# Long feed-forward blocks with their output pieces two and two instead of three and one, and three of the four prepared by adding transfers

## The chip, the cores and the metric

The kernel runs on one core of a Trainium2 chip. The metric is the device time of one execution in microseconds (us); lower is better. Before the change the median of three runs is 2339.63 us (2338.91 to 2342.2).

The core has engines that run side by side, each with its own queue of instructions: TensorE (PE, with its weight loads shown apart as PEld), VectorE (DVE), ScalarE (ACT), GpSimd (POOL) and SyncE (SP). Here SP and POOL mostly issue DMA transfers, which 16 DMA engines carry out.

## The reference

One decoder layer on 256 tokens of width 2048, all in float32. Two SwiGLU feed-forward networks (FFN) stand around a token mixer:

```python
def swiglu(h, w_in, w_out):
    a, b = jnp.split(h @ w_in, 2, axis=-1)
    return (jax.nn.silu(a) * b) @ w_out

h = layer_norm(DN_ALPHA * h + 0.5 * swiglu(h, ffn1_w_in, ffn1_w_out), ln1_g, ln1_b)
...
h = layer_norm(DN_ALPHA * h + merged @ w_out, ln2_g, ln2_b)
h = layer_norm(DN_ALPHA * h + 0.5 * swiglu(h, ffn2_w_in, ffn2_w_out), ln3_g, ln3_b)
```

`w_in` of an FFN is 2048 x 11264, `w_out` is 5632 x 2048. Between the two FFNs stand sparse attention, a gated linear recurrence and their merge; the change does not touch the text of that part. (The mixer's pieces go through the same class of weights.)

## The kernel before

**Three products for one.** TensorE multiplies a rounded float32 format. To keep float32 accuracy every operand is split into a high part (the value rounded) and a low part (what the rounding left out), and a product takes three matmuls: high by high, high by low, low by high (`three`, lines 742 to 745). Activations are split once and kept. Weights stream from memory and are split as they come, in pieces of 128 x 1024 (512 KB).

**How a piece is split.** `Weights` holds the list of all pieces in the order in which TensorE uses them. There are three ways:

- A plain piece: SP loads it into a `raw` tile (four buffers), ACT copies it into the high half of an `hl` tile (five buffers; line 275), DVE subtracts to get the low half (line 276).
- A form: a chunk of 128 x 2048 (1 MB) of an input matrix is not multiplied as it stands but in seven products of sums of blocks, as in Strassen's scheme (42 matmuls of 256 columns instead of 24 of 512). A chunk gives four pieces, `p1q3`, `p2`, `q5p7`, `q4p6`. DVE first makes sums (lines 230, 234, 237 in `operand`), then ACT and DVE split them as above. The chunk itself is a `rf` tile.
- A far piece: its split is made without DVE. ACT copies the piece twice, in halves of 512 columns: minus the rounded value into the low tile (line 182), the rounded value into the high tile (line 185). A DMA on POOL's queue then adds the float32 weights from memory to the low tile (line 183, `accum_op=OP.add`). The four tiles (`wd`) come from the common pool `u` of 53 buffers of 128 x 512.

**When.** `unit` walks through the pieces. At each new piece (`self.cur`) it calls `far_to(cur + 12)`, which loads far pieces up to 16 pieces ahead of use and splits those up to 12 ahead, all eight instructions of one piece at once; then it loads the others up to 8 pieces ahead and splits them up to 4 ahead (`split_to`, bounded by `self.cap`). PE, SP and POOL carry out their instructions in the order of the program's text; the order on ACT and DVE is made by a planner from costs and priorities.

**Blocks.** An FFN has 22 blocks (`blockF`); one gives 256 columns of each half of `h @ w_in`, for all 16 tiles of 128 rows. `gate` then forms silu(a) * b on ACT and DVE (lines 1132 to 1145), and after six pieces of the next block PE transposes it (line 1151), and ACT and DVE split it into two `g` tiles, also of the pool `u`. The blocks form segments (0-1, 2-5, 6-9, 10-13, 14-17, 18-21, in `SEGS`). While one segment is computed, the segment before it is multiplied by its rows of `w_out`, as "output pieces" (`"o"` in a plan, `fill`): four output pieces give one 512-column part, whose sum is copied into a `yd` tile (two buffers, line 1174) and added to memory by a DMA on POOL (line 1175). `OUT_LAST` is the order of the last segment's pieces after block 21.

**Plans.** `block_plan` writes a block's pieces down. A long block (6 to 21) has 20: three output pieces, two chunks of forms (eight pieces), one output piece, two chunks. Of the four output pieces (rows k = 0, 2, 4, 6 of the segment) those with k = 2 and k = 6 are far, in `block_pieces`; k = 0 and k = 4 are plain.

What stands in the pool `u` during the long blocks: 16 tiles of split activations, 16 of their sums for the forms, the `g` tiles (8 of the segment that is consumed, those so far made of the present one) and the `wd` tiles, four for each far piece that is prepared and not yet used up.

Of the kernel before, what the change touches and what calls it, by code (L numbers as in the profile page):

```python
# [11 lines left out]
AF = mybir.ActivationFunctionType  # L12
OP = mybir.AluOpType
# [8 lines left out]
NBK = NKF // 2  # L22
# [38 lines left out]
HL_PITCH = 2112  # L61
BEGINS = (48, 16, 0)
AHEAD = 4
EARLY = 12
LOADS = 4
FORMS = ("p1q3", "p2", "q5p7", "q4p6")
PIECE = 1024
FAST = (0, 1, 2, 3)
# [31 lines left out]
FOUR = tuple(range(6, 22))  # L100


def layer_plans():
    three = (1, 2, 3)
    plans = [block_plan((), 0)] * 2
    plans += [block_plan((1, 3), 2, 0)] + [block_plan(three, 2, 2, late=False)] * 3
    for n in range(6, NBK):
        plans.append(block_plan(FAST if n in FOUR else three, 4, 3))
    return plans


# [1 line left out]
PLANS = layer_plans()  # L113
# [24 lines left out]
class Weights:  # L138
# [8 lines left out]
    def __init__(self, nc, pool, pieces, on_piece):  # L147
        self.nc, self.pool, self.on_piece = nc, pool, on_piece
        self.fast_pool = self.third = None
        self.chunks = 0  # L150
        self.wide = None
        self.pieces = pieces
        self.raw = {}
        self.sums = {}
        self.hl = {}
        self.loaded = 0
        self.split = 0
        self.cur = -1
        self.limit = None
        self.cap = len(pieces)  # L160
        self.off = 0
        self.far = []
        self.apart = ()
        self.far_raw = {}
        self.far_loaded = self.far_split = 0

    def far_to(self, i):


        nc = self.nc  # L170
        while self.far_loaded < len(self.far) and self.far[self.far_loaded] <= i + LOADS:
            k = self.far[self.far_loaded]
            ap = self.pieces[k][0]
            t = self.far_raw[k] = self.pool.tile([P, PIECE], F32, name=f"raw{k}", tag="raw", bufs=RAW_BUFS)
            nc.sync.dma_start(t, ap)
            self.far_loaded += 1
        while self.far_split < len(self.far) and self.far[self.far_split] <= i:
            k = self.far[self.far_split]
            ap, t = self.pieces[k][0], self.far_raw.pop(k)
            h, l = ([self.wide() for _ in range(2)] for _ in range(2))  # L180
            for c in range(2):
                nc.scalar.activation(l[c], t[:, c * 512:(c + 1) * 512], AF.Copy, scale=-1.0)
                nc.gpsimd.dma_start(l[c], ap[:, c * 512:(c + 1) * 512], accum_op=OP.add)
            for c in range(2):
                nc.scalar.activation(h[c], t[:, c * 512:(c + 1) * 512], AF.Copy)
            self.hl[k] = (h, l)
            self.far_split += 1

    def key(self, i):
        ap, form = self.pieces[i]  # L190
# [91 lines left out]
    def unit(self, n):  # L282
        if self.cur < 0 or self.off == self.size(self.cur):
            self.hl.pop(self.cur, None)
            self.cur += 1
            self.off = 0
            self.far_to(self.cur + EARLY)
            self.load_to(self.cur + AHEAD + LOADS)
            self.split_to(self.limit or min(self.cur + AHEAD, self.cap))
            self.on_piece(self.size(self.cur) * (1 if self.pieces[self.cur][1] else 2))  # L290
        h, l = self.hl[self.cur]
        o = self.off
        self.off += n
        assert self.off <= self.size(self.cur)
        if self.cur in self.apart or self.cur in self.far:
            return h[o // 512], l[o // 512]
        return h[:, o:o + n], l[:, o:o + n]
# [70 lines left out]
def tile_layer(ctx, tc, x_fm, x_tm, pos, f1a, f1o, wA, wki, wB, wG, lru, wab, wrb, wo, f2a, f2o,  # L368
               cols_d, ln1_g, ln1_b, ln2_g, ln2_b, ln3_g, ln3_b, out):
    nc = tc.nc  # L370
# [31 lines left out]

    bg = Background()

    pieces, far, apart = [], [], set()

    def keep_apart(n):
        apart.update(range(len(pieces) - n, len(pieces)))
# [6 lines left out]
    def block_pieces(ap, plan, fills=None, fo=None):  # L415
        chunk = {}
        for f, k in plan:
            if f == "c":
                pieces.append((ap[:, k * 512:k * 512 + PIECE], None))
            elif f == "o" and not fo:  # L420
                plain([next(fills)])
            elif f == "o":
                g, nb, k = next(fills)
                if k in (2, 6) and (g or nb >= 2):
                    far.append(len(pieces))
                k += 2 * SEGS[g][0]
                pieces.append((fo[nb][:, k * 512:k * 512 + PIECE], None))
            else:
                if k not in chunk:
                    chunk[k] = ap[:, k * 2048:(k + 1) * 2048]  # L430
                pieces.append((chunk[k], f))
# [30 lines left out]
    for i in range(NR + LAG):  # L462
# [4 lines left out]
        if i >= LAG:  # L467
            g, c = divmod(i - LAG, TPG)
            o = sum(LRU_COLS[:c])
# [14 lines left out]
    keep_apart(WIDE)  # L484

    W = Weights(nc, pool, pieces, bg.paced)
    W.far, W.apart = far, apart
    W.across = {v.tensor.name for v in (wki, wB, lru)}
    W.wide = lambda: U("wd", F32R)
    W.fast_pool = ctx.enter_context(tc.tile_pool(name="f1", bufs=1))  # L490
# [633 lines left out]
    def ffn(x, forms, ln):  # L1124
        def gate(c, e, g, i, lag, plain):

            z = W.fast_pool.tile([P, 4 * S], F32, name=name("z"), tag="z", bufs=Z_BUFS)
            z4 = z.rearrange("p (j c) -> p j c", j=4)
            a, b = z4[:, 0:4:2], z4[:, 1:4:2]
            if e:  # L1130
                p1, p6, p7, q5 = e[0][:, :S], e[0][:, S:], e[1][:, :S], e[1][:, S:]
                A.activation(z4[:, 0], p1, AF.Copy)
                V.tensor_tensor(z4[:, 1], z4[:, 0], p6, op=OP.add)
                V.tensor_tensor(z4[:, 2], z4[:, 1], p7, op=OP.add)
                V.tensor_tensor(b, q5[:, None, :].to_broadcast([P, 2, S]), z4[:, 1:3], op=OP.subtract)
                for t in range(2):
                    w = 512 if plain or t == 0 else S
                    zt = z[:, t * 512:t * 512 + w]
                    V.tensor_tensor(zt, zt, c[t][:, :w], op=OP.add)  # L1139
                A.activation(a, a, AF.Silu)  # L1140
            else:
                for t in range(2):
                    A.activation(z4[:, 2 * t], c[t][:, :S], AF.Silu)
                    A.activation(z4[:, 2 * t + 1], c[t][:, S:], AF.Copy)
            V.tensor_tensor(a, a, b, op=OP.mult)
            for _ in range(lag):
                yield
            ps = BP()
            for k in range(2):
                for t in range(2):  # L1150
                    T.transpose(ps[:, k * S + t * P:k * S + (t + 1) * P], z[:, t * 512 + k * P:t * 512 + (k + 1) * P], ident)
            with tc.high_priority() if lag == LAG_T[1] else nullcontext():
                for k in range(2):
                    hl = UHL("g")
                    split(hl, ps[:, k * S:(k + 1) * S])
                    g[i + k] = hl

        g = [[None] * (2 * (b1 - b0)) for b0, b1 in SEGS]
        fills = iter(FILLS)
        open_ps = []  # L1160
        acc = sums[ln.last]

        def fill():
            s, nb, k0 = next(fills)
            if k0 == 0:
                open_ps[:] = MM(), MM()
            for k in (k0, k0 + 1):
                w = W.unit(512)
                for t in range(2):
                    tokens(open_ps[t], g[s][k], t, w, k == 0, k == len(g[s]) - 1)  # L1170
            if k0 + 2 == len(g[s]):
                for t in range(2):
                    u = W.fast_pool.tile([P, 512], F32, name=name("yd"), tag="yd", bufs=2)
                    A.activation(u, open_ps[t], AF.Copy, scale=0.5)
                    G.dma_start(acc[t][nb], u, accum_op=OP.add)

        for s, (b0, b1) in enumerate(SEGS):
            for n in range(b0, b1):
                c, e = blockF(x, forms, PLANS[n], fill)
                task = gate(c, e, g[s], 2 * (n - b0), LAG_T[n == NBK - 1], ("c", 0) in PLANS[n])  # L1180
                with tc.high_priority():
                    next(task)
                bg.add("gate", task)
        def back():
            for nb in range(4):
                for t in range(2):
                    Y[t][nb] = U("y")
                    G.dma_start(Y[t][nb], acc[t][nb])
                    yield

        bg.add("back", back())
        new_stats((24, 30) if ln.last else (24, 24))
        if not ln.last:
            share("t")
            bg.add("main", later(consts(), W.last.ins))
        out_product(g[-1], ln, pair=True)
# [283 lines left out]
    for nb in range(4):  # L1480
        g, got = got, fetch(ga[nb + 1]) if nb < 3 else None
        s, _ = product(ya, ya_forms, YA_FAST[nb])
# [213 lines left out]
```

## Time and profile before

| | us |
|---|---|
| median of three runs | 2339.63 (2338.91 to 2342.2) |
| the profiled execution | 2340.27 |
| span of its instructions | 2338.4 |
| outside the span | 1.87 |

| engine | busy us | share of the span |
|---|---|---|
| PE | 2312.5 | 99% |
| DVE | 2201.5 | 94% |
| ACT | 1560.0 | 67% |
| POOL | 263.4 | 11% |

The TensorE clock is granted in full all through. Matmuls are pipelined: a matmul's duration overlaps with the next one's, so what counts for PE is the distance from one start to the next, and a PE that is 99% busy may still have room. In the long blocks the trace repeats itself from block to block, so one block can be read for all.

### The profile page before, as it was taken

To read this page: it belongs to the slowest core of one execution; us is meant where nothing else is said; L and a number is where in the kernel's file an instruction comes from. 1 tells how busy PE (TensorE), PEld (TensorE's weight loads), DVE (VectorE), ACT (ScalarE), POOL (GpSimd) and SP (SyncE) were. 2 spreads that over 40 slices of the span, in tenths; PEclk is the share of its full clock that TensorE was granted. 3 is DMA by queue.
4 is the path that set the end of the run, shared out by engine and by line. 5 is a ranking of instruction groups with operands and counts; after the bars stand their busy time and mean duration, and the time that the engine had idled before them with its cause. 6 is when DMAs were issued, how large, how long until landed. Compare 5 with 4: busy or idle time off the path is not lost.

```text
span 2338.4 us, 40427 instructions
## 1 busy us (share of the span) xinstructions
PE 2312.5 (99%) x15430; PEld 2109.4 (90%) x15430; DVE 2201.5 (94%) x3196; ACT 1560.0 (67%) x2273; POOL 263.4 (11%) x368
## 2 busy tenths in 40 slices
PE   9999999999999999999999999999999999999998
PEld 7899999999988999888899998888889999999997
DVE  7999999999999999979887888998999999999997
ACT  7667777777757656556557785555667777777763
POOL 1101111111110000000100001100111111111111
PEclk9999999999999999999999999999999999999999
DMA  9878988888876556554675658655788888888875
GB/s 336 251 238 240 261 250 251 250 256 250 230 244 209 192 187 216 185 189 154 244 239 193 200 182 326 239 198 195 242 275 232 253 255 252 243 252 267 244 221 215
DMA packets 142178, 546.97 MB, mean 234 GB/s; under 512 B 16640, under 2 KB 17280, under 8 KB 117536
## 3 DMA queue, kind: packets, MB, share of 16 engines
q1 hardware_dynamic: 100800, 455.00, 55.1%
q0 software_dynamic: 41040, 89.27, 18.4%
q8 instruction: 120, 1.97, 0.3%
q14 instruction: 74, 0.61, 0.1%
q10 hardware_dynamic: 144, 0.13, 0.0%
HBM read 507.10 MB, written 37.22 MB: 233 GB/s over the span
## 4 chain that ended last, share of the span: by engine, by line
PE 66%; DVE 23%; issue 5%; DMA 3%; ACT 2%; POOL 0%; SPq 0%; ACTq 0%; DVEq 0%; POOLq 0%
PE mm L743 13%; PE mm L745 13%; PE mm L744 13%; DVE hl L276 13%; PE bp L744 5%; PE bp L745 5%; PE bp L743 4%; PE mm L1390 3%; PE mm L1389 3%; PE mm L1391 3%; DVE ws L230 2%; DVE rf L237 2%; DVE rf L234 2%; ACT hl L275 2%; DMA raw<-f1o 1%
## 5 line engine op out<-in xcount | busy, mean ns | idle before, releaser
L275 ACT ACTIVATE hl<-rf 128x1024 fp32r<-128x1024 f32 x573 | 511.3, 912 | 232.9 <-DVE rf L237 119.7
L276 DVE TENSOR_TENSOR hl<-rf,hl 128x1024 fp32r<-128x1024 f32 x573 | 596.9, 1047 | 8.2 <-ACT hl L275 3.8
L276 DVE TENSOR_TENSOR hl<-raw,hl 128x1024 fp32r<-128x1024 f32 (+3 forms) x402 | 474.2, 1196 | 62.2 <-ACT hl L275 61.4
L275 ACT ACTIVATE hl<-raw 128x1024 fp32r<-128x1024 f32 (+3 forms) x402 | 408.4, 1035 | 179.4 <-PE mm L745 82.8
L744 PE MATMUL bp<-hl,sh 128*128 128x256 f32 x1146 | 323.6, 282 | 10.1 <-DVE hl L276 10.1
L743 PE MATMUL bp<-hl,sh 128*128 128x256 f32 x1146 | 320.9, 280 | 0.0
L745 PE MATMUL bp<-hl,sl 128*128 128x256 f32 x1146 | 320.2, 279 | 0.0
L743 PE MATMUL mm<-hl,hs 128*128 128x512 f32 (+1 forms) x800 | 274.5, 343 | 1.6 <-DVE z L1139 0.7
L275 ACT ACTIVATE hl<-ws 128x1024 fp32r<-128x1024 f32 x191 | 202.0, 1058 | 102.7 <-DVE ws L230 71.5
L744 PE MATMUL mm<-hl,hs 128*128 128x512 f32 (+1 forms) x800 | 268.3, 335 | 0.0
L745 PE MATMUL mm<-hl,hs 128*128 128x512 f32 (+1 forms) x800 | 267.9, 335 | 0.1
L230 DVE TENSOR_TENSOR ws<-rf 128x1024 f32<-128x1024 f32 x191 | 233.8, 1224 | 5.4 <-DMA rf<-wrb 1.3
L276 DVE TENSOR_TENSOR hl<-ws,hl 128x1024 fp32r<-128x1024 f32 x191 | 234.2, 1226 | 1.8 <-ACT hl L275 1.7
L744 PEld LDWEIGHTS bp<-hl,sh 128*128 128x128 f32 x1146 | 215.4, 188 | 17.5 <-DVE hl L276 16.3
L745 PEld LDWEIGHTS bp<-hl,sl 128*128 128x128 f32 x1146 | 217.7, 190 | 0.0
L743 PEld LDWEIGHTS bp<-hl,sh 128*128 128x128 f32 x1146 | 215.4, 188 | 1.3
L1389 PE MATMUL mm<-hs,hl 128*128 128x256 f32 x640 | 178.3, 279 | 0.0
L1391 PE MATMUL mm<-hs,hl 128*128 128x256 f32 x640 | 177.8, 278 | 0.0
L1390 PE MATMUL mm<-hs,hl 128*128 128x256 f32 x640 | 177.7, 278 | 0.0
L743 PEld LDWEIGHTS mm<-hl,hs 128*128 128x128 f32 x800 | 150.4, 188 | 19.1 <-issue 2.6
L745 PEld LDWEIGHTS mm<-hl,hs 128*128 128x128 f32 x800 | 151.0, 189 | 16.7 <-DVE hs L937 0.5
L744 PEld LDWEIGHTS mm<-hl,hs 128*128 128x128 f32 x800 | 150.5, 188 | 14.3 <-DVE hl L276 0.2
(360 smaller groups left out, 5897.6 us busy)
## 6 DMA issues: line engine op xcount, KB each, us to landing
rf<-f1a SPq DMA_DIRECT2D x75, 1024.0 KB, 7.7
rf<-f2a SPq DMA_DIRECT2D x75, 1024.0 KB, 7.5
raw<-f1o SPq DMA_DIRECT2D x88, 512.0 KB, 6.6
raw<-f2o SPq DMA_DIRECT2D x88, 512.0 KB, 6.6
raw<-wB SPq DMA_DIRECT2D x80, 512.0 KB, 4.8
raw<-wG SPq DMA_DIRECT2D x54, 512.0 KB, 4.2
ya<-yd POOLq DMA_DIRECT2D x80, 256.0 KB, 7.4
rf<-wA SPq DMA_DIRECT2D x20, 1024.0 KB, 5.5
```

Source lines behind the costliest of these rows:

```text
L230: v.tensor_tensor(t, b[:, 0:4:3], b[:, 1:2].to_broadcast([P, 2, 2, 256]), op=OP.add)
L234: v.tensor_tensor(b[:, 1], t[:, 1], b[:, 0], op=OP.add)
L237: v.tensor_tensor(b[:, 0], b[:, 1], b[:, 2], op=OP.add)
L275: nc.scalar.activation(hp, src, AF.Copy)
L276: self.last = nc.vector.tensor_tensor(lp, src, hp, op=OP.subtract)
L743: T.matmul(ps, xh, w[0], start=start, stop=False)
L744: T.matmul(ps, xh, w[1], start=False, stop=False)
L745: T.matmul(ps, xl, w[0], start=False, stop=stop)
L1389: T.matmul(ps[:, :S], w[0], x[:, 0], start=first, stop=False)
L1390: T.matmul(ps[:, :S], w[0], x[:, 1], start=False, stop=False)
L1391: T.matmul(ps[:, :S], w[1], x[:, 0], start=False, stop=last)
```

## The change

In the long blocks two output pieces stand ahead of two chunks of forms, and two more ahead of the other two chunks. In segments whose output pieces come from `g >= 2` (consumed in blocks 10 to 21) the piece with k = 4 becomes far too, so that three of four are far. Far pieces are begun 14 pieces ahead instead of 12, and those of `g >= 2` are loaded 22 ahead (the others 18) instead of 16. A far piece is made in four steps, one at each new piece of the walk, instead of all at once. Through the last block of an FFN splitting stops two pieces past the block.

```diff
-EARLY = 12
+EARLY = 14
 LOADS = 4
+FAR_LOADS = (4, 8)
...
+def halves(chunks):
+    forms = [(f, q) for q in chunks for f in FORMS]
+    n = len(forms) // 2
+    return 2 * [("o", 0)] + forms[:n] + 2 * [("o", 0)] + forms[n:]
+
 def layer_plans():
...
-        plans.append(block_plan(FAST if n in FOUR else three, 4, 3))
+        plans.append(halves(FAST) if n in FOUR else block_plan(three, 4, 3))
...
     def far_to(self, i):
-        while self.far_loaded < len(self.far) and self.far[self.far_loaded] <= i + LOADS:
+        while (self.far_loaded < len(self.far) and
+               self.far[self.far_loaded] <= i + FAR_LOADS[self.far[self.far_loaded] in self.soon]):
...
         while self.far_split < len(self.far) and self.far[self.far_split] <= i:
             k = self.far[self.far_split]
             ap, t = self.pieces[k][0], self.far_raw.pop(k)
-            h, l = ([self.wide() for _ in range(2)] for _ in range(2))
-            for c in range(2):
-                nc.scalar.activation(l[c], t[:, c * 512:(c + 1) * 512], AF.Copy, scale=-1.0)
-                nc.gpsimd.dma_start(l[c], ap[:, c * 512:(c + 1) * 512], accum_op=OP.add)
-            for c in range(2):
-                nc.scalar.activation(h[c], t[:, c * 512:(c + 1) * 512], AF.Copy)
-            self.hl[k] = (h, l)
             self.far_split += 1
+            self.far_steps.append((k, self.far_copies(k, ap, t)))
+        if self.far_steps:
+            self.far_step()
+
+    def far_copies(self, k, ap, t):
+        nc = self.nc
+        h, l = [], []
+        for c in range(2):
+            l.append(self.wide())
+            nc.scalar.activation(l[c], t[:, c * 512:(c + 1) * 512], AF.Copy, scale=-1.0)
+            nc.gpsimd.dma_start(l[c], ap[:, c * 512:(c + 1) * 512], accum_op=OP.add)
+            yield
+        for c in range(2):
+            h.append(self.wide())
+            nc.scalar.activation(h[c], t[:, c * 512:(c + 1) * 512], AF.Copy)
+            if c == 0:
+                yield
+        self.hl[k] = (h, l)
+
+    def far_step(self):
+        if next(self.far_steps[0][1], self) is self:
+            self.far_steps.popleft()
...
             self.far_to(self.cur + EARLY)
+            while self.far_steps and self.far_steps[0][0] <= self.cur:
+                self.far_step()
...
-                if k in (2, 6) and (g or nb >= 2):
+                if k in (2, 6) and (g or nb >= 2) or k == 4 and g >= 2:
                     far.append(len(pieces))
+                    if g >= 2:
+                        soon.add(len(pieces))
...
             for n in range(b0, b1):
+                if n == NBK - 1:
+                    W.cap = W.cur + len(PLANS[n]) + 2
                 c, e = blockF(x, forms, PLANS[n], fill)
                 task = gate(c, e, g[s], 2 * (n - b0), LAG_T[n == NBK - 1], ("c", 0) in PLANS[n])
                 with tc.high_priority():
                     next(task)
+                W.cap = len(pieces)
                 bg.add("gate", task)
```

More of the change, by code (lines that the diff above doesn't have):

```diff
@@ L162, in __init__ @@
         self.far = []
+        self.soon = ()
         self.apart = ()
@@ L165, in __init__ @@
         self.far_loaded = self.far_split = 0
+        self.far_steps = deque()
     def far_to(self, i):
         nc = self.nc
-        while self.far_loaded < len(self.far) and self.far[self.far_loaded] <= i + LOADS:
+        while (self.far_loaded < len(self.far) and
+               self.far[self.far_loaded] <= i + FAR_LOADS[self.far[self.far_loaded] in self.soon]):
             k = self.far[self.far_loaded]
@@ L403, in tile_layer @@
     bg = Background()
-    pieces, far, apart = [], [], set()
+    pieces, far, apart, soon = [], [], set(), set()
     def keep_apart(n):
@@ L486, in tile_layer @@
     W = Weights(nc, pool, pieces, bg.paced)
-    W.far, W.apart = far, apart
+    W.far, W.apart, W.soon = far, apart, soon
     W.across = {v.tensor.name for v in (wki, wB, lru)}
```

## The prediction

> **What bounds the kernel now.** I read the page first: the engines, and the chain that ended last.
>
> ```profile
> PE 2312.5 (99%) x15430; PEld 2109.4 (90%) x15430; DVE 2201.5 (94%) x3196; ACT 1560.0 (67%) x2273; POOL 263.4 (11%) x368
> PE 66%; DVE 23%; issue 5%; DMA 3%; ACT 2%; POOL 0%; SPq 0%; ACTq 0%; DVEq 0%; POOLq 0%
> ```
>
> The chain changes between PE and DVE. The change touches the long blocks, so the next view is the busy time in stretches of one block each (31.4 us by the distance at which the pattern repeats): a block inside FFN 1, its last block, one inside FFN 2.
>
> ```profile
> core 0: us, PE busy (x) PEld busy (x) DVE busy (x) ACT busy (x) POOL busy (x), PEclk, DMA share, GB/s
> 590.60:622.00 31.40, 31.12 (x222) 29.02 (x222) 31.29 (x39) 22.79 (x33) 5.15 (x6) 1.00 0.85 251
> 622.00:653.40 31.40, 31.12 (x222) 29.02 (x222) 31.28 (x39) 20.23 (x27) 3.55 (x4) 1.00 0.73 213
> 1867.00:1898.40 31.40, 31.01 (x223) 28.91 (x222) 31.29 (x39) 22.80 (x33) 5.30 (x7) 1.00 0.85 250
> ```
>
> DVE is busy for 31.29 of 31.40 us: it sets the pace. ACT has 8.6 us left. Then the waits; of each row: total, times, longest.
>
> ```profile
> PE bp L744 <- DVE hl L276: 10.1, 30, 0.6
> PE mm L745 <- DVE g L879: 0.2, 1, 0.2
> DVE ws L230 <- DMA rf<-f1a: 0.4, 1, 0.4
> SPq L175 <- ACT wd L185: 4.3, 2, 2.7
> ```
>
> PE waits for DVE once in nearly every long block (30 times), for the low half of a form, and DVE hardly ever waits for a transfer. How close behind is PE? Its timeline (start, length) through block 19 of FFN 1:
>
> ```profile
> 559.13 0.28 PE L743 MATMUL bp<-hl,sh 128*128 128x256 f32 x1
> 564.07 0.28 PE L743 MATMUL bp<-hl,sh 128*128 128x256 f32 x1
> 564.56 0.39 PE L744 MATMUL bp<-hl,sh 128*128 128x256 f32 x1 [0.20 <-DVE hl L276]
> 567.29 0.39 PE L743 MATMUL mm<-hl,g 128*128 128x512 f32 x1
> 575.47 0.28 PE L743 MATMUL bp<-hl,xs 128*128 128x256 f32 x1
> 579.00 0.60 PE L1151 MATMUL bp<-ident,z 128*128 128x128 f32 x4
> 579.36 0.37 PE L743 MATMUL mm<-hl,xs 128*128 128x256 f32 x1
> 579.56 0.28 PE L744 MATMUL mm<-hl,xs 128*128 128x256 f32 x1
> 579.91 0.28 PE L744 MATMUL mm<-hl,xs 128*128 128x256 f32 x1
> 585.58 0.39 PE L743 MATMUL mm<-wd,g 128*128 128x512 f32 x1
> ```
>
> Three output pieces (36 matmuls of 512 columns) take 567.29 to 575.47: 0.2272 us each. The 30 matmuls of 256 columns after them take until 579.00: 0.1177 each; the 42 from 559.13 to 564.07 likewise 0.1176. But the 50 from 579.91 to 585.58, after the transposes, take 0.1134 each. So PE has a wide spacing, which it enters from output pieces, and a narrow one, which it enters after transposes or a wait. This decides how much DVE relief is worth.
>
> **The change part by part.**
>
> *The third far piece* takes one subtraction from DVE in blocks 10 to 21 of both FFNs: 24 blocks.
>
> ```profile
> 565.72 2.36 DVE L276 TENSOR_TENSOR hl<-raw,hl 128x1024 fp32r<-128x1024 f32 x2
> 567.99 1.22 DVE L230 TENSOR_TENSOR ws<-rf 128x1024 f32<-128x1024 f32 x1
> 584.13 1.22 DVE L230 TENSOR_TENSOR ws<-rf 128x1024 f32<-128x1024 f32 x1
> 585.27 1.23 DVE L276 TENSOR_TENSOR hl<-rf,hl 128x1024 fp32r<-128x1024 f32 x1
> 586.40 0.69 DVE L234 TENSOR_TENSOR rf<-ws,rf 128x512 f32<-128x512 f32 x1
> 587.00 0.69 DVE L276 TENSOR_TENSOR hl<-rf,hl 128x512 fp32r<-128x512 f32 x1
> 587.61 0.70 DVE L237 TENSOR_TENSOR rf<-rf 128x512 f32<-128x512 f32 x1
> 588.21 1.23 DVE L276 TENSOR_TENSOR hl<-ws,hl 128x1024 fp32r<-128x1024 f32 x1
> 577.12 1.22 DVE L230 TENSOR_TENSOR ws<-rf 128x1024 f32<-128x1024 f32 x1
> ```
>
> Two subtractions cost 567.99 - 565.72 = 2.27, so one costs 1.14, start to start. DVE falls to 31.29 - 1.14 = 30.15 us a block.
>
> *PE then sets the pace.* A block is 48 matmuls of 512 (10.91 us), 168 of 256 and the transposes (579.00 to 579.56: 0.56 with the first matmul after them). In the new order six pieces into a block is the seam between its first and second chunk. The first chunk (42) is wide; the second has its first matmul in the 0.56, then 3 wide and 38 narrow; two output pieces; the last 84 wide. That is 129 x 0.1177 + 38 x 0.1134 = 15.18 + 4.31. Sum: 10.91 + 0.56 + 19.49 = 30.96 us, against 31.40: 0.44 a block, 24 x 0.44 = 10.6 us. DVE's 30.15 and its 0.11 of idle fit with 0.7 us to spare.
>
> *Does DVE keep its lead in the new order?* A chunk costs DVE 1.14 + 1.13 + 0.60 + 0.61 + 0.60 and twice 1.14 = 6.36 us (from the rows), PE 42 x 0.1177 = 4.94. Two chunks on end let it fall 2.8 behind; two output pieces (24 x 0.2272 = 5.45) give that back, as one now stands four pieces ahead at most. Where the block's gate falls (the first pair) the spare is least, about 1 us by my count; a short wait there would put PE into narrow spacing and nearly pay for itself. So a block gains at least 0.28 (the 38 narrow ones wide as well, 38 x 0.0043 = 0.16 less) and at most 0.6 (the second pair narrow after a wait of no length, 42 x 0.0043 = 0.18 more for one chunk). I take 0.42, near the sum, as some blocks will wait a little: 24 x 0.42 = 10.1 us.
>
> *Blocks 6 to 9* keep two plain pieces: same DVE sum, 31.40 as now; between +0.1 and -0.1 each from the order, I take 0.
>
> *What the far piece adds.*
>
> ```profile
> 564.45 1.99 ACT L275 ACTIVATE hl<-raw 128x1024 fp32r<-128x1024 f32 x2
> 583.56 1.14 ACT L182 ACTIVATE wd<-raw 128x512 fp32r<-128x512 f32 x2
> 584.60 1.14 ACT L185 ACTIVATE wd<-raw 128x512 fp32r<-128x512 f32 x2
> 584.47 1.75 POOL L183 DMA_DIRECT2D wd<-f1o x2 [21.80 <-PE bp L745]
> 560.45 5.70 SPq L216 DMA_DIRECT2D rf<-f1a  x2
> rf<-f1a SPq DMA_DIRECT2D x75, 1024.0 KB, 7.7
> wd<-f1o POOLq DMA_DIRECT2D x68, 256.0 KB, 9.5
> ```
>
> ACT: four copies at 0.52 for one at 0.95, +1.1 us, to 23.9 of 31.0; hidden by its idle time. POOL: two more issues, +1.8 on 5.2; hidden. DMA: the last block prepares no far pieces and shows a share of 0.73 against 0.85, so a far piece costs about 0.06 and the share becomes 0.92 (estimate from these two rows). What hides that: a chunk's load issued at 560.45 is first read at 577.12, 16.7 us later, and needs 7.7; landing could take 9 us more before DVE waits. Without that cover each microsecond is one on DVE, of which 0.7 are free. I take 0. The Trainium skill's page "DMA: Bandwidth & Descriptors", section "Issuing engines are not separate DMA queues", speaks against the change here: transfers of POOL and SP run on the same 16 DMA engines and interleave. The rows agree (the share falls with POOL's transfers), but by the 9 us of slack the rule costs nothing.
>
> *Earlier loads, spread steps.* On SP the raw loads move ahead of about two chunk loads; there are four raw buffers, and SP's 4.3 us of waiting for far copies is today's price. A chunk load held up by one output piece (2.7 us) is still inside the 9 us. On POOL the adding DMAs, now one at each piece, stand in the same line as the `yd` transfers; a blocked one holds those back, but the next part's `yd` is eight forms (about 10 us) later. On ACT single copies stand ahead of form copies instead of four at once (2.1 us). From -0.1 to +0.1 a block, taken as 0.
>
> *The cap in block 21* moves two subtractions of plain pieces behind the gate's first steps; three then come within the first output piece, 3.4 us for pieces needed 5.5 us later. The wait on `g` that it may shorten is 0.2 in all. Taken as 0.
>
> Sum: 2340.27 - 10.1 = 2330.2 for an execution like the profiled one, with 2326 to 2333.5 by the bounds of the block. The median before lies 0.6 below that execution, so I say **2330**.
>
> **The rivals.**
>
> *No change* (15%): DVE's saved time becomes waiting for ACT inside the chunk pairs, and the pace stays at 31.2 to 31.4. For it: the planner, not the text, orders ACT and DVE. Against: 0.7 us to spare and ACT at 77%. 24 x 0.1 = 2 us: 2338.
>
> *Slower: the pool of 53 tiles* (10%). By my count of the text, splits and forms hold 32, `g` up to 12, two far pieces 8: 52. With three and the earlier start it is 12 `wd` tiles, 56 in the second to fourth block of a segment, 18 of the 24. Then a copy, or a `g` tile, waits on ACT until PE has used the piece with k = 4, and form copies stand behind it. The wait is at most that piece (2.7 us), at least nothing, since the copies have ten pieces until their use. If half of it (1.4) reached PE, the 18 blocks would take 30.96 + 1.4 = 32.4: +17, less 6 x 0.44, 2354. It turns the sign from 24 x 0.44 / 18 = 0.6 us a block.
>
> *Faster: PE always in narrow spacing* (8%). With all 168 at 0.1134 PE needs 10.91 + 0.56 + 19.0 = 30.5 us; 24 x 0.9 = 21.6: 2319. For it: every wait before a form sets PE to narrow until the next output piece. Against: in the rows the unbroken stretches behind output pieces are wide, and with DVE ahead there are fewer waits.
>
> *Faster: no floor of PE in reach* (3%). If the spacing itself came from the shortage at DVE (matmuls that trickle, not PE's own rate), DVE would go on setting the pace, at 30.15 + 0.11 = 30.26 us: 24 x 1.14 = 27.4, 2313. Against: the 36 matmuls of 512 keep 0.2272 throughout while their operands lie ready. [...]
>
> **How the numbers follow.** Forecast 64% (2325 to 2335 alone), no change 15%, slower 10%, the two faster cases 11%. A measurement of this kernel tells about 0.2% (4.7 us) from no change. Faster: 64 + 11 less 1 for small gains, 74%; same 15%; slower 11%. The range, from 2318 (PE always narrow) to 2340 (no change), leaves out the slower case, the fastest one and the edges of the others, under 2 in 10.
>
> **What would show it.** Right: blocks 10 to 21 at 30.9 to 31.05 us, DVE about 30.15 in them, no PE wait for `hl` (or a short one), blocks 6 to 9 at 31.4, DMA share near 0.92. Wrong: DVE idle with PE waiting (order or pool), ACT waiting for PE before `wd` copies, DVE waiting for `rf`, or 256-column matmuls at 0.1134 after output pieces.

## The result and the profile after

The changed kernel takes 2352.6 us (median of four runs, 2351.35 to 2353.6), the kernel before, run beside it, 2339.45 (2338.91 to 2342.2). The ratio is 1.0051, with an interval of 1.0039 to 1.0064: slower by half a per cent, where 2330 was forecast, and outside the range. The span of the profiled execution grew from 2338.4 to 2349.6 us. One execution of a kernel below (the one with all steps of a far piece at once) took 3818.98 us at a granted clock of 0.655 and is left out of that kernel's figures.

First the page of the kernel after, its engines and the chain that ended last:

```profile
PE 2317.6 (99%) x15430; PEld 2114.1 (90%) x15430; DVE 2183.9 (93%) x3172; ACT 1594.1 (68%) x2345; POOL 305.9 (13%) x416
PE 66%; DVE 23%; issue 5%; ACT 3%; DMA 2%; POOL 0%; SPq 0%; ACTq 0%; DVEq 0%; POOLq 0%
```

The 24 subtractions are gone (3196 DVE instructions became 3172) and DVE is busy for 18 us less. The chain's shares are almost those of before, so the page alone doesn't tell what went wrong. The windows of one block inside each FFN do (columns as in the prediction's table of windows):

```profile
419.90:451.40 31.50, 31.06 (x220) 29.00 (x220) 30.20 (x37) 24.20 (x35) 7.11 (x8) 1.00 0.94 267
2017.00:2048.50 31.50, 31.08 (x221) 29.04 (x221) 30.66 (x38) 24.19 (x35) 7.11 (x8) 1.00 0.93 266
```

DVE needs 30.20 us in the first of them, as forecast, and 30.66 in the second, yet each takes 31.5. DVE has 1.3 and 0.8 us of room, ACT seven, and the block is no shorter: something is waited for. The view of the waits names it (total, times, longest):

```profile
PE mm L772 <- DVE z L1168: 12.3, 22, 1.2
...
ACT wd L200 <- PE mm L773: 10.2, 7, 1.6
...
ACT wd L200 <- DMA raw<-f1o: 5.4, 3, 3.1
...
ACT wd L200 <- DMA raw<-f2o: 5.1, 3, 3.9
...
PE bp L773 <- DVE hl L301: 2.8, 5, 0.7
```

The wait that was to go has gone: PE waits for the low half of a form 5 times instead of 30. Two kinds of waits have taken its place. PE now waits for DVE's work on `z`, a tile that the waiting matmul doesn't read; 20 of these 22 waits stand in long blocks, 0.40 to 0.86 us each. And ACT waits for far pieces that have not landed. (ACT also waits for PE before it makes far copies, 10.2 us; that row is taken up with the rivals.) In the kernel before, the first of these rows read as follows, two waits for `raw<-f1o` had 0.5 us in all, and one for `raw<-f2o` had 2.1:

```profile
PE mm L743 <- DVE z L1139: 0.7, 2, 0.5
ACT wd L182 <- DMA raw<-f1o: 0.5, 2, 0.3
```

**The wait for `z`.** Here is PE's timeline after, from the end of one long block into the next:

```profile
381.83 0.39 PE L772 MATMUL mm<-hl,g 128*128 128x512 f32 x1
...
387.27 0.28 PE L772 MATMUL bp<-hl,xs 128*128 128x256 f32 x1
...
387.86 0.28 PE L774 MATMUL bp<-hl,xs 128*128 128x256 f32 x1
388.54 0.36 PE L772 MATMUL mm<-hl,sh 128*128 128x256 f32 x1 [0.40 <-DVE z L1168]
```

and DVE's beside it:

```profile
383.05 0.41 DVE L1162 TENSOR_TENSOR z<-z,bp 128x256 f32<-128x256 f32 x1
383.38 1.22 DVE L301 TENSOR_TENSOR hl<-ws,hl 128x1024 fp32r<-128x1024 f32 x1
384.51 0.41 DVE L1163 TENSOR_TENSOR z<-z,bp 128x256 f32<-128x256 f32 x1
384.84 1.22 DVE L301 TENSOR_TENSOR hl<-rf,hl 128x1024 fp32r<-128x1024 f32 x1
385.98 0.68 DVE L1164 TENSOR_TENSOR z<-bp,z 128x512 f32<-128x512 f32 x1
386.58 1.22 DVE L255 TENSOR_TENSOR ws<-rf 128x1024 f32<-128x1024 f32 x1
387.71 1.01 DVE L1168 TENSOR_TENSOR z<-z,mm 128x512 f32<-128x512 f32 x2
```

A block ends at 381.83, where the output pieces of the next begin. Its sums stand in accumulator banks, which the gate has to read (line 1168 reads `c[0]`, then `c[1]`). The seventh matmul of the first form, `mm<-hl,sh`, starts a new sum in the bank of `c[0]`; PE could start it at 387.86 + 0.12 = 387.98, which is 6.15 us after the block's end (24 matmuls of output pieces and six of the form). DVE does the gate's five operations between form work. The row of line 1168 holds two of them, of 0.68 and 0.41 us; the first, which reads `c[0]`, ends at 387.71 + 0.68 = 388.39, 6.56 us after the block's end, and PE starts at 388.54, 0.56 late. In the kernel before, the same two places were these:

```profile
572.72 1.02 DVE L1139 TENSOR_TENSOR z<-z,mm 128x512 f32<-128x512 f32 x2
...
576.17 0.28 PE L743 MATMUL mm<-hl,sh 128*128 128x256 f32 x1
```

There, the block had ended at 567.29: the bank was needed 8.88 us later and `c[0]` had been read 6.11 us later (572.72 + 0.68). The third output piece was worth 2.7 us of cover, and the new order took it away. The Trainium skill's page "Perfetto Trace Analysis", section "Matmuls", asks that independent groups rotate through the banks, so that the reading of one overlaps the next group's matmuls; the trace agrees, as here the first sum of the new block falls on a bank that is still being read, and starts 0.56 us late.

**The far pieces that have not landed.** In block 3 of FFN 1, SP's load of a far piece (line 185) and what it issued ahead of it:

```profile
77.90 0.33 SPq L241 DMA_DIRECT2D raw<-f1a  x1
88.62 0.33 SPq L241 DMA_DIRECT2D rf<-f1a  x1
89.01 0.46 SPq L185 DMA_DIRECT2D raw<-f1o  x1
```

and ACT:

```profile
98.21 0.63 ACT L200 ACTIVATE wd<-raw 128x512 fp32r<-128x512 f32 x1 [3.05 <-DMA raw<-f1o]
98.75 1.56 ACT L300 ACTIVATE hl<-rf 128x1024 fp32r<-128x1024 f32 x2
```

SP issues in the order of the text, and it stood for 10.3 us at the chunk load of 88.62, until DVE was through with that load's tile; the far piece's load came behind it. ACT takes up the copy before this load has landed, 9.2 us after its issue, and the form copies behind it wait for 3.05 us too.

**Where the 11.2 us lie.** The table gives distances between the first transposes of the gates, in us, worked out from the traces of all kernels; a block's figure runs from six pieces into it to six pieces into the next. The mixer's text is the same in all.

```
                          FFN 1                                FFN 2
                 blk 2-4  5-9    10-20 (one)     21   mixer   2-4    5-9    10-20 (one)     21
before            80.28  151.01  345.85 (31.44) 33.45 992.31  81.80 151.36  345.41 (31.40) 33.33
after             84.11  150.71  347.11 (31.56) 34.18 993.74  84.35 151.25  347.30 (31.57) 34.18
e1_three_first    87.06  151.73  339.90 (30.90) 33.59 991.94  84.78 152.29  340.69 (30.97) 33.23
e2_order_alone    81.41  151.15  345.45 (31.40) 34.40 991.07  82.43 151.83  345.45 (31.40) 34.36
e3_early_as_b.    80.35  150.70  347.66 (31.61) 34.17 993.23  81.44 152.47  347.67 (31.61) 34.17
e4_bank_freed     89.85  154.16  344.20 (31.29) 34.42 990.91  86.60 151.75  342.52 (31.14) 35.70
e5_three_f._12    80.56  151.66  339.90 (30.90) 33.44 991.37  80.89 152.59  339.90 (30.90) 32.82
e6_three_f._8     80.64  151.84  340.42 (30.95) 33.30 991.65  84.72 152.94  340.63 (30.97) 33.46
e7_third_alone    79.83  151.50  343.98 (31.27) 33.70 993.49  81.89 152.33  343.56 (31.23) 34.08
e8_everywhere     80.71  149.66  339.90 (30.90) 33.04 991.97  81.49 150.05  341.11 (31.01) 32.81
e9_at_once        80.93  151.62  343.85 (31.26) 34.62 992.44  82.62 152.28  343.72 (31.25) 33.92
e10_no_cap        79.69  149.66  339.90 (30.90) 32.81 992.68  81.90 150.09  339.90 (30.90) 32.81
e11_freed_12      85.06  153.58  342.88 (31.17) 34.43 990.49  84.53 154.85  341.69 (31.06) 35.24
```

Blocks 10 to 20 lost 0.1 to 0.2 us each instead of gaining 0.44 (+1.3 and +1.9 us in all), blocks 2 to 4 lost 3.8 and 2.6, block 21 lost 0.7 and 0.85, the mixer 1.4. The mixer varies by 3.2 us from kernel to kernel with no edit in it, and what sets that was not looked into.

### The profile page after: what moved, and what is told of

Read it like the earlier page. It is cut to its first block, busy times and chain, and to the rows that moved or that the text cites. A ratio compares the mean times of both kernels' runs of the same rounds, so it can differ in the third digit from the quotient of the medians.

```text
span 2349.6 us, 40575 instructions
## 1 busy us (share of the span) xinstructions
PE 2317.6 (99%) x15430; PEld 2114.1 (90%) x15430; DVE 2183.9 (93%) x3172; ACT 1594.1 (68%) x2345; POOL 305.9 (13%) x416
## 4 chain that ended last, share of the span: by engine, by line
PE 66%; DVE 23%; issue 5%; ACT 3%; DMA 2%; POOL 0%; SPq 0%; ACTq 0%; DVEq 0%; POOLq 0%
PE mm L772 13%; PE mm L773 13%; PE mm L774 13%; DVE hl L301 13%; PE bp L773 4%; PE bp L772 4%; PE bp L774 4%; PE mm L1421 3%; PE mm L1423 3%; PE mm L1422 3%; DVE ws L255 3%; ACT hl L300 2%; DVE rf L262 2%; DVE rf L259 1%; DVE z L1168 1%
## 5 line engine op out<-in xcount | busy, mean ns | idle before, releaser
L301 DVE TENSOR_TENSOR hl<-raw,hl 128x1024 fp32r<-128x1024 f32 (+2 forms) x378 | 446.9, 1192 | 67.9 <-ACT hl L300 67.0
L300 ACT ACTIVATE hl<-raw 128x1024 fp32r<-128x1024 f32 (+2 forms) x378 | 386.8, 1034 | 178.1 <-PE mm L774 84.6
```

The costliest lines, as they stand in the source:

```text
L300: nc.scalar.activation(hp, src, AF.Copy)
L301: self.last = nc.vector.tensor_tensor(lp, src, hp, op=OP.subtract)
```

## The experiments

Three parts could be at fault: the order two and two, the earlier start of the far pieces with its loads, and the third far piece with its spread steps. Each was undone or done alone. Each ratio is to runs of the kernel before that were taken beside it.

### The old order, with all the rest of the change

```diff
-        plans.append(halves(FAST) if n in FOUR else block_plan(three, 4, 3))
+        plans.append(block_plan(FAST if n in FOUR else three, 4, 3))
```

> The changed kernel with the old order in the long blocks (three output pieces first, one in the middle); all else as changed. Theory A (accumulator): with two output pieces first, PE reaches the first matmul into the accumulator bank that the gate of the block before still reads 6.2 us after that block's end, and DVE has read it only after 6.6 to 7.1 us; with three pieces first PE comes 2.7 us later and never waits. So blocks 10 to 21 fall from about 31.6 to 30.95 us: 24 x 0.65 = 15 less, about 2337. Theory B (tile pool and queues: 12 wd tiles and earlier loads hold up ACT or SP): nothing is relieved, 2350 to 2353.

Measured: 2338.77 us (2336.91 to 2342.02), ratio 0.9997 (0.9987 to 1.0006). Blocks 10 to 20 of FFN 1 take 30.90 us each, against 31.56 with the new order: the wait for the bank goes when three output pieces stand ahead again. What keeps it from gaining is in blocks 2 to 4, which lose 6.8 and 3.0 us. Its waits:

```profile
ACT wd L200 <- DMA raw<-f1o: 8.4, 2, 5.0
...
ACT wd L200 <- DMA raw<-f2o: 7.1, 3, 4.6
...
PE mm L772 <- DVE z L1168: 3.1, 4, 1.1
```

ACT's waits for raw far pieces are even longer than in the changed kernel (longest 5.0 and 4.6 us, against 3.1 and 3.9).

### The new order alone, in the kernel before

```diff
-        plans.append(block_plan(FAST if n in FOUR else three, 4, 3))
+        plans.append(halves(FAST) if n in FOUR else block_plan(three, 4, 3))
```

> The kernel before with nothing but the new order (two output pieces, two chunks, twice), two far pieces as before. Theory A: PE waits for the accumulator bank in all 32 long blocks, but DVE sets the pace there anyway, so blocks stay at 31.4 to 31.6: 2340 to 2346, with waits of PE for the gate's sums in the trace. Theory B: the order costs nothing, 2338 to 2341, no such waits.

Measured: 2342.56 us, ratio 1.0011 (1.0002 to 1.0020): the time is in the range of theory A, but the waits that it names are not there. The long blocks stay at 31.40, where PE is held back at the forms (second row); PE's two waits for `z` both stand in block 5:

```profile
PE mm L749 <- DVE z L1145: 1.7, 2, 1.1
...
PEld mm L750 <- DVE hl L282: 7.5, 35, 0.7
```

PE wants the bank as early as in the changed kernel, but DVE has read it sooner. From the end of a block at 380.75:

```profile
383.38 0.68 DVE L1141 TENSOR_TENSOR z<-bp,z 128x512 f32<-128x512 f32 x1
383.98 0.68 DVE L243 TENSOR_TENSOR rf<-rf 128x512 f32<-128x512 f32 x1
384.57 1.00 DVE L1145 TENSOR_TENSOR z<-z,mm 128x512 f32<-128x512 f32 x2
```

```profile
386.91 0.28 PE L749 MATMUL mm<-hl,sh 128*128 128x256 f32 x1
```

`c[0]` has been read at 384.57 + 0.68, 4.50 us after the block's end, and PE comes to the bank after 6.16. Here form operations of 0.68 us stand between those of the gate, in the changed kernel some of 1.22. The wait belongs to the two edits together: the order brings PE's need from 8.88 to 6.15 us, and with the third far piece DVE's reading comes at 6.56 instead of 4.50.

### The far pieces begun and loaded as before, the rest of the change kept

```diff
-EARLY = 14
+EARLY = 12
-FAR_LOADS = (4, 8)
+FAR_LOADS = (4, 4)
```

> The changed kernel with far pieces begun 12 pieces ahead and loaded 16 ahead, as before. Theory A: only the stretch of blocks 2 to 6 answers, where the changed kernel lost 2.9 us in the first network and 2.1 in the second: about 2347, blocks 10 to 21 still at 31.5 with the wait. Theory B: the pressure on the pool is gone, blocks 10 to 21 fall below 31.2: 2340 or less.

Measured: 2346.93 us (2345.94 to 2349.14), ratio 1.0032 (1.0020 to 1.0045), 5.7 us below the changed kernel. Blocks 2 to 4 come back to 80.35 and 81.44; the longer wait of ACT for `raw<-f1o` is gone, and the wait for the bank is all there:

```profile
PE mm L772 <- DVE z L1168: 12.6, 26, 0.9
...
ACT wd L200 <- DMA raw<-f1o: 1.5, 2, 0.8
```

So the earlier start is one loss, the order the other, and they stand side by side.

### The bank freed sooner

A copy on ACT at the head of the gate takes `c[0]` out of its bank, and DVE adds from the copy.

```diff
+                u = W.fast_pool.tile([P, 512], F32, name=name("cz"), tag="yd", bufs=2)
+                A.activation(u, c[0], AF.Copy)
                 A.activation(z4[:, 0], p1, AF.Copy)
...
-                    V.tensor_tensor(zt, zt, c[t][:, :w], op=OP.add)
+                    V.tensor_tensor(zt, zt, c[t][:, :w] if t else u, op=OP.add)
```

On the changed kernel:

> The changed kernel, order and all, but the gate first copies its first accumulator bank to a tile by ACT (0.58 us) and DVE adds from that copy, so the bank is free about 1 us after the block's end. Theory A: the wait at the first matmul into the bank is gone and blocks 10 to 21 come to 31.0 (0.6 less each, up to 0.1 back for ACT): about 2338. Theory B: no better than 2352, or worse for the added copy.

Measured: 2357.22 us, ratio 1.0075 (1.0060 to 1.0090). The total was missed by far. Blocks 11 to 20 do fall, to between 30.93 and 31.56 us, but blocks 2 to 10 lose more. The same copy with the far pieces begun and loaded as before:

> The changed kernel with its own order (two and two), far pieces begun 12 and loaded 16 ahead, and the gate's first accumulator bank copied out by ACT at once. Theory A: with the stalls of blocks 2 to 4 and the wait for the bank both gone, blocks 10 to 21 at 30.9 to 31.1, so 2347 - 24 x 0.5 = 2335 or less, though the added copy (0.58 us of ACT, and a tile shared with the output sums) may take some back in blocks 2 to 9. Theory B: 2346 or more.

Measured: 2350.41 us, ratio 1.0041 (1.0027 to 1.0055); missed too. Yet the block that the copy was to mend is mended. One window of it, and three of its waits:

```profile
404.00:434.90 30.90, 30.90 (x221) 29.02 (x220) 30.26 (x38) 24.01 (x36) 6.96 (x8) 1.00 0.95 269
```

```profile
PE mm L772 <- DVE z L1170: 5.5, 2, 4.8
...
PE mm L772 <- ACT yd L1205: 3.2, 1, 3.2
...
ACT cz L1162 <- DMA ya<-yd: 28.8, 16, 8.0
```

With the order two and two, blocks 11 to 18 take 30.95 us each in both FFNs, against 31.44 to 32.08 without the copy, and PE is busy throughout the window. So the late reading of the bank is what held them. The copy has a price elsewhere: its tile is one of the two `yd` tiles, which wait for output sums on their way to memory (the third row, 28.8 us). In block 2 the copy waits so for 7.2 us in FFN 1 and 8.0 in FFN 2, PE then for 4.8 and 3.2, and the block is 6.3 and 4.6 us longer than before. How the price in the other blocks divides between the shared tiles and ACT's longer queue wasn't separated.

### The old order, far pieces begun and loaded as before

Both losses taken away; the third far piece, the spread steps and the cap stay.

```diff
-EARLY = 14
+EARLY = 12
-FAR_LOADS = (4, 8)
+FAR_LOADS = (4, 4)
...
-        plans.append(halves(FAST) if n in FOUR else block_plan(three, 4, 3))
+        plans.append(block_plan(FAST if n in FOUR else three, 4, 3))
```

> The changed kernel with three output pieces first and far pieces begun 12 and loaded 16 ahead, as before; the third far piece, the spread steps and the cap stay. Theory A with its second part (copies put into ACT's order before their raw piece has landed hold ACT in blocks 2 to 4, 6 us in the first network and 3.5 in the second): both losses gone, blocks 10 to 21 at 30.9, so 2340.0 - 22 x 0.5 = 2329. Theory B (the third far piece's tiles and transfers themselves cost): not under 2335.

Measured: 2329.97 us (2328.89 to 2330.09), ratio 0.9954 (0.9941 to 0.9968), as expected. One block of each FFN:

```profile
419.90:450.80 30.90, 30.90 (x222) 29.02 (x221) 30.43 (x37) 23.76 (x35) 7.03 (x8) 1.00 0.94 273
2017.00:2047.90 30.90, 30.90 (x223) 29.02 (x222) 30.43 (x38) 23.76 (x36) 7.03 (x9) 1.00 0.94 273
```

PE is busy for the whole of both windows, and all of blocks 10 to 20 take 30.90 us: this is PE's own floor.

### The old order, far pieces begun early but also loaded early

```diff
-FAR_LOADS = (4, 8)
+FAR_LOADS = (8, 8)
...
-        plans.append(halves(FAST) if n in FOUR else block_plan(three, 4, 3))
+        plans.append(block_plan(FAST if n in FOUR else three, 4, 3))
```

> Three output pieces first, far pieces begun 14 ahead, and now all of them loaded 8 pieces before they are begun (4 for those of the first segments in the changed kernel). If the late landing holds ACT, blocks 2 to 4 lose their 6 and 3.5 us only if the earlier load is also issued earlier: 2330 to 2333. If it is the place of the copies in ACT's order as such, or SP cannot issue the load earlier, blocks 2 to 4 stay as slow: 2338 to 2340.

Measured: 2334.65 us (2333.0 to 2335.54), ratio 0.9974 (0.9965 to 0.9983), between the two forecasts. With four pieces more between load and copy, blocks 2 to 4 of FFN 1 fall from 87.06 to 80.64 us, so there it was the late landing: the load of that far piece now goes out at 79.14, ahead of the chunk load at which SP stands until 90.54. In FFN 2 they keep 84.72, nearly all of the loss, though ACT waits there only once for a far piece (1.8 us). It waits 5.2 us, in two waits, for a `yd` tile on its way to memory, against 1.9 in one with the later start (the experiment before); whether that is the loss was not tested.

### The third far piece alone, in the kernel before

```diff
-                if k in (2, 6) and (g or nb >= 2):
+                if k in (2, 6) and (g or nb >= 2) or k == 4 and g >= 2:
```

> The kernel before with nothing but the third far piece (k = 4 of the segments from g = 2): old order, begun 12 and loaded 16 ahead, all eight instructions at once, no cap. If the third piece alone gives the gain: 2329 to 2331, blocks 10 to 21 at 30.9. If the spread steps are needed (four copies at once, 2.1 us of ACT, before the form copies): blocks at 31.1 to 31.4, 2333 to 2339.

Measured: 2340.06 us, ratio 0.9999 (0.9990 to 1.0008), above both forecasts: nothing gained, though the blocks in the middle of a segment take 30.9 to 31.1 us. Those at the edge of a segment (9, 13, 17) take 32.0 to 32.5, and the first of the next one (10, 14, 18) 31.2 to 31.5. The next experiment shows why.

### All steps of a far piece at once

The kernel with the old order and the old start, with the spreading taken out:

```diff
-        if self.far_steps:
+        while self.far_steps:
             self.far_step()
```

> The three-pieces-first version (third far piece, begun 12 ahead, cap) with the eight instructions of a far piece issued at once instead of one step per piece. If the spreading is what lets the third far piece pay: as the kernel with the third piece alone, 2338 to 2341, with runs of four or eight far copies on ACT and PE waiting for forms. If it was the cap or chance: 2330.

Measured: 2340.52 us (median of nine, 2338.12 to 2342.61), ratio 0.9996 (0.9987 to 1.0006), about 10.5 us above the same kernel with spread steps. (A far piece is four copies and two adding transfers, so six instructions and not eight.) ACT in block 14 of FFN 1, the first of a segment:

```profile
425.56 1.15 ACT L200 ACTIVATE wd<-raw 128x512 fp32r<-128x512 f32 x2
426.60 1.14 ACT L205 ACTIVATE wd<-raw 128x512 fp32r<-128x512 f32 x2
427.64 0.62 ACT L300 ACTIVATE hl<-rf 128x512 fp32r<-128x512 f32 x1
428.17 1.14 ACT L200 ACTIVATE wd<-raw 128x512 fp32r<-128x512 f32 x2
429.21 1.14 ACT L205 ACTIVATE wd<-raw 128x512 fp32r<-128x512 f32 x2
430.25 1.04 ACT L300 ACTIVATE hl<-ws 128x1024 fp32r<-128x1024 f32 x1
```

and what DVE has to wait for after it:

```profile
431.33 1.23 DVE L301 TENSOR_TENSOR hl<-ws,hl 128x1024 fp32r<-128x1024 f32 x1 [1.14 <-ACT hl L300]
```

At the edge of a segment two far pieces come close together: eight copies with one short form copy between them, 4.7 us, while DVE waits 1.14 us for a form's high half. It had 30.90 - 30.43 = 0.47 us to spare, 0.67 less than that wait, and the block takes 31.53, 0.63 more than PE's floor. Block 13 has the same heap at 394.15: DVE waits 1.68 us, and the block takes 31.95. With the steps spread, the same place has form copies after two copies at most:

```profile
424.28 1.14 ACT L200 ACTIVATE wd<-raw 128x512 fp32r<-128x512 f32 x2
425.32 1.05 ACT L300 ACTIVATE hl<-ws 128x1024 fp32r<-128x1024 f32 x1
426.27 1.14 ACT L205 ACTIVATE wd<-raw 128x512 fp32r<-128x512 f32 x2
427.31 2.00 ACT L300 ACTIVATE hl<-rf 128x1024 fp32r<-128x1024 f32 x2
```

PE's waits for the low half of a form are 21 in the one kernel and 5 in the other.

### Three far pieces from block 6 on

On the old order and the old start:

```diff
-                if k in (2, 6) and (g or nb >= 2) or k == 4 and g >= 2:
+                if k in (2, 6) and (g or nb >= 2) or k == 4 and g >= 1:
```

> As e5, with the third far piece in blocks 6 to 9 too (g = 1). Theory A: eight more blocks fall from 31.4 to 30.9 to 31.0, 3 to 4 us under e5: about 2326. If the pool of 53 tiles binds anywhere it is here, at the start of the long blocks: no better than e5, with ACT waiting for PE before far copies.

Measured: 2325.31 us (2322.82 to 2327.08), ratio 0.9935 (0.9922 to 0.9947). Blocks 8 and 9, which still had two plain pieces, fall to 30.90 as well:

```profile
233.00:263.90 30.90, 30.90 (x223) 29.02 (x221) 30.42 (x38) 24.11 (x35) 7.03 (x8) 1.00 0.94 273
```

```profile
ACT wd L200 <- PE mm L774: 7.8, 8, 1.0
```

This kernel asks for the most tiles of all, and ACT does wait for PE to give some back, eight times, 1.0 us at most; its blocks stay at PE's floor (all but one of those from 8 to 20: block 13 of FFN 2 has 32.11, where PE waits 0.9 us for an adding transfer; the same block has 30.90 in the next kernel).

### The same without the cap in block 21

```diff
-                if n == NBK - 1:
-                    W.cap = W.cur + len(PLANS[n]) + 2
```

> The version with the third far piece in all long blocks, without the cap in the last block. If the cap is worth nothing: 2325 within 1 us. If it shortens the end of each network: up to 2 us more.

Measured: 2324.2 us (2323.56 to 2325.9), ratio 0.9932 (0.9919 to 0.9944). The cap is worth nothing that can be measured here. This is the fastest kernel of the study: faster than the one before by 0.7% and than the changed one by 1.2%.

## Why the prediction was wrong, point by point

**DVE's relief: right in kind, too large in size.** Forecast 30.15 us a block, measured 30.20 and 30.66 in two blocks of the changed kernel and 30.43 in the old order. Over the program DVE's busy time fell by 17.6 us, where 24 x 1.14 = 27.4 was counted.

**PE's pace: right where PE was let run.** The sum gave 30.96 us; blocks 11 to 18 of the kernel with the freed bank and the later start, the same order, take 30.95. The two spacings are there too: in its block from 418.38, 37 distances of 0.1134 us behind the transposes and 127 of 0.1178, nearly the 38 and 129 of the sum. In the old order the floor is 30.90.

**"Does DVE keep its lead in the new order?": the step that failed.** It counted DVE's work for the forms and said that where the gate falls the spare is least, about 1 us, and that a short wait would nearly pay for itself. It looked at whether forms would be ready, and never asked when PE needs the gate's banks back. The rows for it were quoted: output pieces from 567.29, the first form at 575.47. With one output piece less PE comes to the bank 2.7 us sooner, 8.9 - 2.7 = 6.2 us after the block's end, and the gate's DVE row, which the prediction doesn't show, has read it after 6.1. So the rows of before showed that the cover was gone, but not the size of the wait: the reading moved, to 4.50 us with the order alone and to 6.56 in the changed kernel. The wait costs 0.56 us where it was read, and the blocks 10 to 20 lie 31.57 - 30.96 = 0.6 above the sum on the mean; 22 such blocks give 13.4 us, more than the 24 x 0.42 = 10.1 forecast as gain. Nor did the wait pay for itself: a narrow chunk after it is worth 42 x 0.0043 = 0.18.

**"Earlier loads, spread steps … taken as 0": failed at both ends.** The earlier start costs 5.7 us (the changed kernel against the one begun as before), all of it outside the blocks that the prediction looked at. It weighed what a late transfer does to a chunk load that has 9 us of slack, and not to a copy that ACT takes up in order, with form copies behind it. On SP it saw the raw loads move ahead of chunk loads; the one that was read above stood behind one. The spreading is worth about 10.5 us and had been valued at nothing. Without it the third far piece brings nothing, as the copies of two pieces meet at the edges of segments. "Single copies stand ahead of form copies instead of four at once" named the very thing, with 2.1 us as the most that could stand in a row; at the edges it is twice that.

**The cap: taken as 0, right.** **ACT, POOL and the DMA share: right.** Forecast 23.9 us, 7.0 us and 0.92, measured 24.2, 7.11 and 0.94, with nothing late in the long blocks for it.

**The rivals.** Slower came, but not by the pool of 53 tiles. Its sign did show: ACT waits for PE before far copies, 10.2 us in seven waits (second of its rows of waits above). But it waits so in the fast kernel of the old order and the old start too (six times, 1.0 us at most), and the kernel that asks for the most tiles has blocks of 30.90 us; and in the rows beside the wait for the bank DVE is never idle, so what came late there was held up by DVE's own work. "No change" had the pace nearly right (31.2 to 31.4 us a block, measured 31.56), but with the cause in ACT instead of the banks. PE always narrow wasn't seen, nor was a PE without a floor: the floor of 30.90 us stood in every kernel in which PE ran free, with DVE at 30.43.

The forecast total, 2330, is what the third far piece with spread steps gives without the order and the earlier start (2329.97). That is no support for the path by which it was reached: the sum was made for the new order.

## What to carry to other kernels

When work is moved out from between two uses of an accumulator bank, compare two times from the end of the group: when the last reader of the bank is through, and when the first matmul of the next group wants it. The first of them shifts with whatever work stands between the reader's operations (4.50 to 7.02 us here), so an edit that costs little alone (0.11% here) may eat the gain of another. A copy whose input comes by DMA holds up what stands behind it on its engine (3.05 us here), so it belongs after the landing, and a few at a time between the copies that the matmuls wait for. A load is issued no earlier than the loads ahead of it in its queue.

## What the hardware showed that was not expected

PE's pace is steadier than the prediction allowed for: in the old order with the old start 22 blocks took 30.90 us each, to 0.01, and at a DMA share of 0.94 of all 16 engines no wait of PE for a transfer stood in these blocks.

Loads of one size take very different times to land. The view of the DMA issues (queue, times, KB, median us from issue to landing), for the output pieces of FFN 1 in the changed kernel, where the kernel before has 6.6:

```profile
raw<-f1o SPq DMA_DIRECT2D x88, 512.0 KB, 8.0
```

The changed kernel has 92 adding transfers there instead of 68, but their number alone is not the reason: the kernel with all steps at once has 92 too and a median of 6.6, the one with the third far piece alone 6.7. With the steps spread it lies between 6.8 and 9.1, and the two fastest kernels have the slowest loads (9.0 and 9.1), and no engine waits for a transfer in their blocks 10 to 20 of FFN 1. The chunks of twice the size went from 7.7 before to 6.2 in the changed kernel. What sets these times was not separated.
